# Two transformer blocks on one core: the routing query's norm factor moves from a VectorE multiply into the exponent, and the routing indices stay integers

## The chip, the cores and the metric

The kernel runs on one core of a Trainium2 chip. The metric is the device time of one execution in microseconds (us); smaller is better. Five engines run side by side, each working through its own list of instructions in a fixed order: TensorE (PE: matrix multiplies; its loads of stationary operands are counted apart, as PEld), VectorE (DVE), ScalarE (ACT), GpSimd (POOL) and SyncE (SP, which issues most transfers). An instruction that needs another engine's result waits for a semaphore, and all that stands behind it on its own engine waits with it.

## The reference

One sequence of 512 tokens, width 1024, goes through two transformer blocks in float32. The change lies in the last part of the second block, a feed-forward layer that picks 128 of 16,384 experts for each token. Cut to that part:

```python
def peer(h, w_pq, sub_keys, u_emb, v_emb):          # h: the normalised input, 512 x 1024
    q = (h @ w_pq).reshape(B, S, 8, 2, 128)         # 8 heads, two half-queries each
    sc = jnp.einsum("bshcd,hcnd->bshcn", q, sub_keys)        # 128 scores for each half
    s_top, i_top = lax.top_k(sc, 16)
    cand = s_top[..., 0, :, None] + s_top[..., 1, None, :]   # 16 x 16 sums
    cand_idx = i_top[..., 0, :, None] * 128 + i_top[..., 1, None, :]
    ...
    best, pos = lax.top_k(cand, 16)
    expert_idx = jnp.take_along_axis(cand_idx, pos, axis=-1)
    gate = jax.nn.softmax(best, axis=-1)
    ...
    a = gelu(einsum("ced,cd->ce", u_emb[idx], hx))           # per chunk of 128 tokens
    return einsum("ce,ced->cd", g * a, v_emb[idx])
```

The normalised input is h = x * r * g, where r is one factor for each token (one over the root mean square) and g a gain for each of the 1024 columns. r is positive, so scores with and without it have the same order within a token.

## The kernel before

**Weights.** Every matrix product runs over weight units w0 to w435 of 128x1024. A unit is brought from HBM by SP, two units to a transfer, and split into a high part (`w..h`, an ACT copy) and a low part (`w..l`, a subtraction); a product is then three matmuls (hi*lo, lo*hi, hi*hi). There are three buffers for split units, so a unit's copy on ACT may run only a little ahead of PE. The low part is made on DVE, or, for units 180 to 307 while the planner's flag `gates_on` is off, on POOL (`lo_eng`).

**Routing.** w164 to w179 are the 16 products `pq{h}{c}` (8 heads, two halves), 128x512 in PSUM with the queries along the partitions and the tokens along the columns. Each is carried to SBUF as `pqs` by a DVE multiply with `rr[1]`, the factors r spread over all partitions (`n4r` in the trace). For each head `head_lists` makes the 128 scores of 512 tokens on PE (`sk`), copies them to SBUF on ACT (`skc`), and finds the 16 best of each half with `top16` on DVE: for each of four token blocks two rounds of MAX8 and FIND_INDEX8, with a MATCH_REPLACE8 between them. The positions come as 32-bit integers in `iu` and are cast to bfloat16 in `itop_`. `pqs` and `skc` share a pool of seven 128x512 buffers (`t2`).

**From lists to gates.** `block_best(b)`, b = 0 to 3, takes one block of 128 tokens: it adds candidate scores, picks the best 16, takes the positions apart, looks up the list indices with a one-hot product (`eq`, 128x1024, four times a block), and makes the softmax gate (`best`, `bsum`, `IJG`). Block 0 goes by rows: for each of 128 choices a gathered row of U and of V (POOL gathers, `last`/`row<-in_un` and `in_vn`; DVE reduces, printed as ISA or CUSTOM). Blocks 1 to 3 go by dense tables: `gates()` turns IJG round on PE (`ijg`), splits it into bfloat16 parts (`ijb`, `grest`), and for every 8 tokens builds five one-hot tiles on DVE (`hot`, a set of five; a name such as `hot_3120` is block 3, token 120, and a set's buffers are two deep, one of the five only one). From each set PE makes two groups `gp` of 12 small matmuls (4 tokens each), ACT copies a group to `stage`, and every fourth group a 1 MB transfer `g_dr` writes the table out. All in all 48 sets and 96 groups. Meanwhile PE runs the products `u` over w180 to w307 (24 matmuls of 128x384 to a unit), whose results are multiplied with the tables and with w308 to w435 in the last stage (`acc`).

**What sets the order.** All engines' lists are fixed when the program is built, by a planner. `Clock` keeps a modelled time for each engine; `Merge` runs the main line (weights and products) and weaves in steps of the side lines: `ls` (head lists, block_best, gates, one after the other), `rw` (rows), `ln` (norms). A step of a side line says when it is due: `room("V", 1.5)` is the time at which modelled DVE work has shrunk to 1.5 us ahead. The modelled price of a DVE operation is

```python
two = all(x.dtype == BF16 for x in (out, *ins))
return 0.07 + n / (1920 if two else 960)
```

for n elements a partition. One place ends the weaving: before the product of w304 (`o == NOCT - 1 and j == 4` in `peer_u`) `yield ("ls",)` lets out all that is left of the lists and gates, without a product between.

Of the kernel before, what the change touches and what calls it, by code (L numbers as in the profile page):

```python
# [10 lines left out]
F32 = mybir.dt.float32  # L11
F32R = mybir.dt.float32r
BF16 = mybir.dt.bfloat16
I32 = mybir.dt.int32
U32 = mybir.dt.uint32
AF = mybir.ActivationFunctionType
ALU = mybir.AluOpType
# [4 lines left out]
P = 128  # L22
# [3 lines left out]
NB = 4  # L26
# [164 lines left out]
def body(tc, a):  # L191
# [5 lines left out]
    with ExitStack() as ctx:  # L197
# [121 lines left out]
        wk = mkpool(ph, "wk")  # L319
# [4 lines left out]
        def t2(name, dt=F32):  # L324
            return wk.tile([P, T], dt, tag="t2", name=name, bufs=NT2)
# [228 lines left out]
        rr = []  # L554
# [205 lines left out]
        for g in range(2):  # L760
            c = 64 * g
# [318 lines left out]
        def u_rows():  # L1080

            due = clk.free["PE"]
            while rows[0] < P:
# [2 lines left out]
                due = max(due + PACE, clk.free["PE"] - 2 * PACE)  # L1086
                row_step()
                yield due
        iota = wk.tile([P, P], F32, name="iota")
        G.iota(iota, pattern=[[1, P]], base=0, channel_multiplier=0, allow_small_or_imprecise_dtypes=True)  # L1090
        iota2 = wk.tile([P, P, 2], BF16, name="iota2")
        V.tensor_copy(iota2, iota[:, :, None].to_broadcast([P, P, 2]))


        stop_ = wk.tile([P, 2, NB, 8, 16], F32, name="stop_")
        itop_ = wk.tile([P, 2, NB, 8, 16], BF16, name="itop_")
        iu = wk.tile([P, NB, 16], U32, name="iu")
        IJG = wk.tile([P, NB, 3, P], F32, name="IJG")
        iota16 = wk.tile([P, 16, 16], BF16, name="iota16")
        V.tensor_copy(iota16, iota[:, 0:16, None].to_broadcast([P, 16, 16]))  # L1100

        def top16(vals, idx, x):

            V.max(vals[:, 0:8], x)
            V.max_index(idx[:, 0:8], vals[:, 0:8], x)
            V.match_replace(x, vals[:, 0:8], x, -3.0e38)
            V.max(vals[:, 8:16], x)
            V.max_index(idx[:, 8:16], vals[:, 8:16], x)
# [10 lines left out]
        def head_lists(h, qs):  # L1119
            sk = skeys.pop(0)  # L1120
            load_sk(h + 2)
            yield at(*qs)
            for c in range(2):
                s_ = psd(f"sk{h}{c}")
                for b in range(NB):
                    PE.matmul(s_[:, b * P:(b + 1) * P], qs[c][:, b * P:(b + 1) * P], sk[:, c, :],
                              start=True, stop=True)
                sc = t2(f"skc{h}{c}")
                S.activation(sc, s_, AF.Copy)
                yield room("V", 1.5, sc)  # L1130
                for b in range(NB):
                    top16(stop_[:, c, b, h], iu[:, b], sc[:, b * P:(b + 1) * P])
                    yield room("V", 1.5)
                V.tensor_copy(itop_[:, c, :, h], iu)

# [4 lines left out]
        def block_best(b):  # L1142

            s0, s1 = stop_[:, 0, b], stop_[:, 1, b]
            ca = wk.tile([P, 8, NCAND], F32, tag="ca", name=f"ca{b}", bufs=1)
            for rows, cols, part in ((slice(0, NFULL), 16, ca[:, :, :NC1]), (slice(NFULL, 16), 4, ca[:, :, NC1:])):
                n = rows.stop - rows.start
                V.tensor_tensor(part.rearrange("p h (i j) -> p h i j", j=cols),
                                s0[:, :, rows, None].to_broadcast([P, 8, n, cols]),
                                s1[:, :, None, :cols].to_broadcast([P, 8, n, cols]), ALU.add)  # L1150
            best = wk.tile([P, 2, 8, 16], F32, tag="best", name=f"best{b}", bufs=1)
            pos = wk.tile([P, 5, 8, 16], U32, tag="pos", name=f"pos{b}", bufs=1)
            for h in range(8):
                top16(best[:, 0, h], pos[:, 0, h], ca[:, h])
                yield room("V", 1.5)

            V.tensor_tensor(best[:, 1], best[:, 0], best[:, 0, :, 0:1].to_broadcast([P, 8, 16]), ALU.subtract)
            S.activation(best[:, 1], best[:, 1], AF.Exp)
            gates_on[0] = True

            for k, (n, op) in enumerate(((4, ALU.logical_shift_right), (15, ALU.bitwise_and),
                                         (2, ALU.logical_shift_right), (3, ALU.bitwise_and))):
                V.tensor_scalar(pos[:, 1 + k], pos[:, 0], n, None, op)
            far = wk.tile([P, 8, 16], F32, tag="far", name=f"far{b}", bufs=1)
            V.tensor_scalar(far, pos[:, 0], float(NC1), None, ALU.is_ge)
            d = wk.tile([P, 2, 8, 16], F32, tag="dpos", name=f"dpos{b}", bufs=1)
            V.scalar_tensor_tensor(d[:, 0], pos[:, 3], float(NFULL - NC1 // 4), pos[:, 1], ALU.add, ALU.subtract)
            V.tensor_tensor(d[:, 1], pos[:, 4], pos[:, 2], ALU.subtract)
            V.tensor_tensor(d, d, far[:, None].to_broadcast([P, 2, 8, 16]), ALU.mult)
            ab = wk.tile([P, 2, 8, 16], BF16, tag="pab", name=f"pab{b}", bufs=1)  # L1170
            V.tensor_tensor(ab, d, pos[:, 1:3], ALU.add)
            yield room("V", 1.5)
            for c in range(2):

                for h in (slice(0, 4), slice(4, 8)):
                    eq = wk.tile([P, 4, 16, 16], BF16, tag="eq", name=f"eq{b}{c}{h.start}", bufs=1)
                    V.tensor_tensor(eq, ab[:, c, h, None, :].to_broadcast([P, 4, 16, 16]),
                                    iota16[:, None].to_broadcast([P, 4, 16, 16]), ALU.is_equal)
                    V.tensor_tensor(eq, eq, itop_[:, c, b, h, :, None].to_broadcast([P, 4, 16, 16]), ALU.mult)
                    for n in (8, 4, 2):  # L1180
                        V.tensor_tensor(eq[:, :, :n], eq[:, :, :n], eq[:, :, n:2 * n], ALU.add)
                    V.tensor_tensor(IJG[:, b, c].rearrange("p (h k) -> p h k", h=8)[:, h], eq[:, :, 0], eq[:, :, 1],
                                    ALU.add)
                    yield room("V", 1.5)
            sm = wk.tile([P, 2, 8], F32, tag="bsum", name=f"bsum{b}", bufs=1)
            V.tensor_reduce(sm[:, 0], best[:, 1], axis=AX.X, op=ALU.add)
            V.reciprocal(sm[:, 1], sm[:, 0])
            V.tensor_tensor(IJG[:, b, 2].rearrange("p (h k) -> p h k", h=8), best[:, 1],
                            sm[:, 1, :, None].to_broadcast([P, 8, 16]), ALU.mult)
            gates_on[0] = False  # L1190
            if b == 0:
                V.scalar_tensor_tensor(eid, IJG[:, 0, 0], float(P), IJG[:, 0, 1], ALU.mult, ALU.add)
                V.tensor_copy(eg, IJG[:, 0, 2])
                mg.spawn("rw", u_rows())
            yield room("V", 1.5)
# [63 lines left out]
        def peer_u():  # L1259
            mg.spawn("ln", rms_steps(acc, "n4", rr))  # L1260
            for h in range(8):
                qs = []
                for c in range(2):
                    o = yield from linear(hp, f"pq{h}{c}")
                    if h + c == 0:
                        yield ("ln",)
                        mg.spawn("ln", norm2())
                    t = t2(f"pqs{h}{c}")
                    V.tensor_tensor(t, o, rr[1], ALU.mult)
                    qs.append(t)  # L1270
                mg.spawn("ls", head_lists(h, qs))
            yield ("ln",)
            hp.clear()
            cur_n.clear()

            for i in range(2):
                s_ = slot(f"last{i}").rearrange("p k t -> p (k t)")
                acts.append(s_[:, :KT * TD].rearrange("p (k t) -> p k t", k=KT))
                bufs_.append(s_[:, KT * TD:])
            bufs_.extend(rowp.tile([P, D], F32, name=f"row{i}") for i in range(NROW - 2))  # L1280
            for b in range(NB):
                mg.spawn("ls", block_best(b))
            mg.spawn("ls", gates())
            for o in range(NOCT):
                ao = acts[o % 2]
                if o >= NOCT - NRES:
                    aocts[o] = ao
                for j in range(8):
                    if o == NOCT - 1 and j == 4:
                        yield ("ls",)  # L1290
                        last_phase()
                    if o == NOCT - 1 and j == 7:
                        for i in range(WAHEAD):
                            list(weighted(i))
                    r = yield from linear(h2, f"u{o}{j}")
                    S.activation(ao[:, j], r[:, P:], AF.Gelu)
                if o < NOCT - NRES:
                    nc.scalar.dma_start(a_dr[o], ao)
# [242 lines left out]
```

## Time and profile before

| | us |
|---|---|
| median of 3 runs | 2441.09 |
| lowest, highest | 2439.46, 2441.44 |
| profiled execution, its own time | 2439.86 |
| its span in the trace | 2437.8 |
| PE busy in it | 2364.7 (97%) |
| DVE busy in it | 1759.3 (72%) |
| ACT, POOL busy in it | 1036.0 (42%), 741.0 (30%) |

The trace holds every instruction of one execution with its start, its duration and what it waited for. The views used below are sums of busy time by stretch, groups of like instructions, timelines of one engine, and the list of PE's waits. "Granted clock" (PEclk) is TensorE's clock in a stretch as a share of its full speed of 2.4 GHz; 0.50 is its lower level of 1.2 GHz.

### The profile page before, as it was taken

The numbers are of one execution on the slowest core, as the hardware profiler recorded it, in microseconds if no ns is written. First come the engines' busy times: TensorE is split into PE (matmuls) and PEld (weight loads), VectorE is DVE, ScalarE is ACT, GpSimd is POOL, SyncE is SP. The second block draws the span as 40 slices with busy tenths as digits, with TensorE's granted clock in tenths as the row PEclk, the third lists the DMA queues.
The fourth block names the chain that finished last, engine by engine and source line by source line (L and its number), as shares of the span: only waits on it lengthen the run. The fifth ranks groups of instructions, "written<-read, shape, count | busy, mean of one in ns | idle before, by whom it ended". The sixth has DMA issues, their size and how long they took to land.

```text
span 2437.8 us, 33926 instructions
## 1 busy us (share of the span) xinstructions
PE 2364.7 (97%) x13114; PEld 2111.2 (87%) x13121; DVE 1759.3 (72%) x3167; ACT 1036.0 (42%) x1558; POOL 741.0 (30%) x586
## 2 busy tenths in 40 slices
PE   9999999999999889999999999999998999999997
PEld 7777888888776667777889999999997999999997
DVE  4637644443357789755789898999996888888874
ACT  4454433232246456444324334455554333333333
POOL 2122011110126578401233455333322332323211
PEclk9999999999999999999999999999999999999998
DMA  4110222222211112222224788899998999999972
GB/s 169 57 54 35 91 97 93 104 87 104 87 67 55 52 53 87 87 87 91 93 94 173 292 316 301 313 327 347 345 323 265 360 359 364 353 362 355 372 292 85
DMA packets 141857, 466.14 MB, mean 191 GB/s; under 512 B 10624, under 2 KB 61952, under 8 KB 112000
## 3 DMA queue, kind: packets, MB, share of 16 engines
q1 hardware_dynamic: 52416, 281.04, 31.5%
q0 software_dynamic: 36864, 134.23, 15.5%
q10 hardware_dynamic: 52416, 48.70, 5.9%
q8 instruction: 103, 1.69, 0.3%
q14 instruction: 58, 0.48, 0.1%
HBM read 414.65 MB, written 49.28 MB: 190 GB/s over the span
## 4 chain that ended last, share of the span: by engine, by line
PE 66%; issue 14%; DVE 10%; POOL 4%; ACT 3%; DMA 2%; SPq 0%; POOLq 0%; DVEq 0%; ACTq 0%
PE acc L134 22%; PE u L134 9%; PE up L134 5%; PE gate L134 5%; PE pq L134 3%; PE wo L134 2%; PE qkb L134 2%; DVE hot L134 2%; PE co L134 2%; PE gc L134 2%; POOL row L1054 1%; POOL last L1054 1%; PE ga L134 1%; PE ao L134 1%; DVE cyp L134 1%
## 5 line engine op out<-in xcount | busy, mean ns | idle before, releaser
L134 POOL TENSOR_TENSOR cy<-cy,cvt 128x511 f32<-128x511 f32 (+14 forms) x120 | 173.5, 1445 | 69.7 <-ACT cvt L134 59.1
L134 ACT ACTIVATE last<-u 128x384 f32<-128x384 f32 x128 | 63.0, 492 | 226.1 <-PE u L134 225.9
L1054 POOL DMA_INDIRECT last<-in_un,eid x64 | 80.5, 1257 | 167.9 <-DVE ea L134 131.4
L1054 POOL DMA_INDIRECT last<-in_vn,eid x64 | 70.8, 1106 | 198.9 <-DVE yt L134 188.6
L1054 POOL DMA_INDIRECT row<-in_un,eid x64 | 82.3, 1285 | 136.4 <-DVE ea L134 133.5
L1054 POOL DMA_INDIRECT row<-in_vn,eid x64 | 74.1, 1158 | 153.5 <-DVE yt L134 143.6
L134 ACT ACTIVATE stage<-gp 128x512 f32<-128x512 f32 x96 | 95.9, 1110 | 8.0 <-PE gp L134 8.0
L134 DVE TENSOR_TENSOR hot<-hot,ijb 128x1024 bf16<-128x1024 bf16 x144 | 91.0, 686 | 1.5
L134 PE MATMUL gp<-hot,hot 128*128 128x128 bf16 x1152 | 76.0, 221 | 14.1 <-ACT last L134 6.7
L134 PEld LDWEIGHTS <-hot 128*128 128x128 bf16 x1152 | 67.5, 98 | 24.0 <-DVE hot L134 19.6
L134 DVE SCALAR_TENSOR_TENSOR cyp<-u,par,cyp 128x511 f32<-128x511 f32 (+28 forms) x116 | 85.3, 735 | 2.4
L134 DVE CUSTOM_DVE_ANT_0 last<-last,h2tok 128x1024 f32<-128x1024 f32 x64 | 77.2, 1212 | 10.6 <-DMA last<-in_un,eid 10.6
L134 DVE SCALAR_TENSOR_TENSOR yt<-last,ea,yt 128x1024 f32<-128x1024 f32 x63 | 80.5, 1278 | 2.1 <-DMA last<-in_vn,eid 2.1
L134 DVE SCALAR_TENSOR_TENSOR yt<-row,ea,yt 128x1024 f32<-128x1024 f32 x64 | 81.8, 1278 | 0.1
L134 DVE CUSTOM_DVE_ANT_0 row<-row,h2tok 128x1024 f32<-128x1024 f32 x64 | 77.2, 1213 | 5.7 <-DMA row<-in_un,eid 5.3
L134 ACT ACTIVATE cvt<-u,par 128x511 f32<-128x511 f32 (+14 forms) x120 | 78.9, 700 | 0.0
L134 DVE TENSOR_TENSOR wv<-last,goct 128x384 f32<-128x384 f32 x128 | 70.5, 551 | 0.0
L134 DVE TENSOR_TENSOR hot<-iota,ijb 128x1024 bf16<-128x1024 bf16 x96 | 61.7, 683 | 0.0
L134 DVE TENSOR_TENSOR su<-up,n2r 128x512 f32<-128x512 f32 x22 | 15.2, 691 | 51.8 <-PE up L134 51.8
L134 PEld LDWEIGHTS o<-v,pT 128*128 128x128 f32 x224 | 29.6, 199 | 18.4 <-DVE pT L134 10.9
L134 PE MATMUL o<-v,pT 128*128 128x64 f32 x224 | 31.8, 284 | 10.7 <-DVE pT L134 7.6
L134 DVE MAX8 stop__8676<-skc 128x8 f32<-128x128 f32 x128 | 36.8, 287 | 5.5 <-ACT skc L134 3.2
(6459 smaller groups left out, 8465.9 us busy)
## 6 DMA issues: line engine op xcount, KB each, us to landing
raw<-in_w SPq DMA_DIRECT2D x89, 1024.0 KB, 4.8
raw<-in_u SPq DMA_DIRECT2D x64, 1024.0 KB, 7.4
raw<-in_v SPq DMA_DIRECT2D x64, 1024.0 KB, 7.2
g_dr<-stage ACTq DMA_DIRECT2D x24, 1024.0 KB, 8.4
goct<-g_dr SPq DMA_DIRECT2D x64, 384.0 KB, 8.8
a_dr<-last ACTq DMA_DIRECT2D x14, 1536.0 KB, 9.9
last<-a_dr SPq DMA_DIRECT2D x56, 384.0 KB, 10.3
xT<-in_x_t SPq DMA_DIRECT2D x1, 1024.0 KB, 9.5
```

The source lines that it names most:

```text
L134: return f(*args, **kw)
L1054: nc.gpsimd.indirect_dma_start(row_buf(n), None, t, bass.IndirectOffsetOnAxis(ap=eid[:, n % P:n % P + 1], axis=0))
```

## The change

The queries are carried to SBUF by a plain ACT copy, without r. The lists are then made on scores without r, and r comes in where `best` goes through the exponential on ACT, as its scale, one value for each token (a token is a partition there). FIND_INDEX8 writes into `itop_`, now of 32-bit integers, and the 16 casts and `iu` are gone, so the `eq` product has one bfloat16 and one 32-bit operand. The mask `far` and one 128x256 product become two operations of 128x128 that compare and multiply. `iota` borrows a `t2` buffer until it has been read.

```diff
--- before.py
+++ after.py
@@ -1086,18 +1086,18 @@
                 due = max(due + PACE, clk.free["PE"] - 2 * PACE)
                 row_step()
                 yield due
-        iota = wk.tile([P, P], F32, name="iota")
+        iota = t2("iota")[:, :P]
         G.iota(iota, pattern=[[1, P]], base=0, channel_multiplier=0, allow_small_or_imprecise_dtypes=True)
         iota2 = wk.tile([P, P, 2], BF16, name="iota2")
         V.tensor_copy(iota2, iota[:, :, None].to_broadcast([P, P, 2]))
 
 
         stop_ = wk.tile([P, 2, NB, 8, 16], F32, name="stop_")
-        itop_ = wk.tile([P, 2, NB, 8, 16], BF16, name="itop_")
-        iu = wk.tile([P, NB, 16], U32, name="iu")
+        itop_ = wk.tile([P, 2, NB, 8, 16], U32, name="itop_")
         IJG = wk.tile([P, NB, 3, P], F32, name="IJG")
         iota16 = wk.tile([P, 16, 16], BF16, name="iota16")
         V.tensor_copy(iota16, iota[:, 0:16, None].to_broadcast([P, 16, 16]))
+        iota = None
 
         def top16(vals, idx, x):
 
@@ -1129,9 +1129,8 @@
                 S.activation(sc, s_, AF.Copy)
                 yield room("V", 1.5, sc)
                 for b in range(NB):
-                    top16(stop_[:, c, b, h], iu[:, b], sc[:, b * P:(b + 1) * P])
+                    top16(stop_[:, c, b, h], itop_[:, c, b, h], sc[:, b * P:(b + 1) * P])
                     yield room("V", 1.5)
-                V.tensor_copy(itop_[:, c, :, h], iu)
 
 
 
@@ -1155,18 +1154,17 @@
                 yield room("V", 1.5)
 
             V.tensor_tensor(best[:, 1], best[:, 0], best[:, 0, :, 0:1].to_broadcast([P, 8, 16]), ALU.subtract)
-            S.activation(best[:, 1], best[:, 1], AF.Exp)
+            S.activation(best[:, 1], best[:, 1], AF.Exp, scale=rr[0][:, b:b + 1])
             gates_on[0] = True
 
             for k, (n, op) in enumerate(((4, ALU.logical_shift_right), (15, ALU.bitwise_and),
                                          (2, ALU.logical_shift_right), (3, ALU.bitwise_and))):
                 V.tensor_scalar(pos[:, 1 + k], pos[:, 0], n, None, op)
-            far = wk.tile([P, 8, 16], F32, tag="far", name=f"far{b}", bufs=1)
-            V.tensor_scalar(far, pos[:, 0], float(NC1), None, ALU.is_ge)
             d = wk.tile([P, 2, 8, 16], F32, tag="dpos", name=f"dpos{b}", bufs=1)
             V.scalar_tensor_tensor(d[:, 0], pos[:, 3], float(NFULL - NC1 // 4), pos[:, 1], ALU.add, ALU.subtract)
             V.tensor_tensor(d[:, 1], pos[:, 4], pos[:, 2], ALU.subtract)
-            V.tensor_tensor(d, d, far[:, None].to_broadcast([P, 2, 8, 16]), ALU.mult)
+            for c in range(2):
+                V.scalar_tensor_tensor(d[:, c], pos[:, 0], float(NC1), d[:, c], ALU.is_ge, ALU.mult)
             ab = wk.tile([P, 2, 8, 16], BF16, tag="pab", name=f"pab{b}", bufs=1)
             V.tensor_tensor(ab, d, pos[:, 1:3], ALU.add)
             yield room("V", 1.5)
@@ -1265,8 +1263,9 @@
                     if h + c == 0:
                         yield ("ln",)
                         mg.spawn("ln", norm2())
+
                     t = t2(f"pqs{h}{c}")
-                    V.tensor_tensor(t, o, rr[1], ALU.mult)
+                    S.activation(t, o, AF.Copy)
                     qs.append(t)
                 mg.spawn("ls", head_lists(h, qs))
             yield ("ln",)
```

PE's list has the same 13,330 entries before and after. The places at which side work stands change on all engines. The planner's price of an `eq` product goes from 0.07 + 1024/1920 = 0.60 to 0.07 + 1024/960 = 1.14 us, since its operands are no longer all BF16. With that one price left at 0.60 the changed code is built with its `bsum` and `gp` at the old places.

**ACT at the end of the routing products.** Names: `w179h` to `w183h` are high parts of weights, `skc` copies of scores, `last<-u` results of the first products behind the routing. Before:

```order
L134 ACTIVATE w179h<-raw_9212 128x1024
L134 ACTIVATE skc_9387<-sk_9382 128x512
L134 ACTIVATE w180h<-raw_9304 128x1024
L134 ACTIVATE w181h<-raw_9304 128x1024
L134 ACTIVATE skc_9467<-sk_9462 128x512
L134 ACTIVATE w182h<-raw_9398 128x1024
L134 ACTIVATE skc_9546<-sk_9541 128x512
L134 ACT_TABLE_LOAD
L134 ACTIVATE last_9504<-u_9508 128x384
L134 ACTIVATE w183h<-raw_9398 128x1024
```

After:

```order
L134 ACTIVATE pqs_9338<-pq_9290 128x512
L134 ACTIVATE w179h<-raw_9198 128x1024
L134 ACTIVATE pqs_9379<-pq_9340 128x512
L134 ACTIVATE w180h<-raw_9291 128x1024
L134 ACTIVATE skc_9395<-sk_9390 128x512
L134 ACTIVATE pqs_9436<-pq_9381 128x512
L134 ACTIVATE w181h<-raw_9291 128x1024
L134 ACTIVATE skc_9462<-sk_9457 128x512
L134 ACTIVATE pqs_9489<-pq_9438 128x512
L134 ACTIVATE w182h<-raw_9382 128x1024
L134 ACTIVATE skc_9537<-sk_9532 128x512
L134 ACT_TABLE_LOAD
```

The last four query copies now stand among the high parts of w179 to w182. `pqs_9338` waits for head 3's first scores on PE, which stand behind the product of w177; the other three wait for a `t2` buffer until DVE has finished a list: `pqs_9379` that of head 2's second half, `pqs_9436` that of head 3's first, `pqs_9489` that of head 3's second half. On DVE w179's low part stands in the middle of the list of head 2's second half, with two of its four blocks behind it. On PE the scores of head 3's second half stand within the product of w179 and those of head 4's first half within that of w180, before and after.

**DVE where block 3's routing ends**, before (the gate is finished behind the low part of w252) and after (behind that of w268). `ISA` with `ea` is a row reduce:

```order
L134 TENSOR_TENSOR w252l<-raw_12317,w252h 128x1024
L134 ISA last_9504,ea<-last_9504,h2tok 128x1024
L134 ISA ea 128x1
L134 TENSOR_REDUCE bsum_12416<-best_11847 128x8
L134 RECIPROCAL bsum_12416<-bsum_12416 128x8
L134 TENSOR_TENSOR IJG<-best_11847,bsum_12416 128x128
```

```order
L134 TENSOR_TENSOR w268l<-raw_12832,w268h 128x1024
L134 TENSOR_REDUCE bsum_12920<-best_12158 128x8
L134 RECIPROCAL bsum_12920<-bsum_12920 128x8
L134 TENSOR_TENSOR IJG<-best_12158,bsum_12920 128x128
L134 ISA last_9492,ea<-last_9492,h2tok 128x1024
```

The four places of `bsum` are behind w204l, w221l, w237l and w252l before, and behind w205l, w226l, w247l and w268l after. On POOL the low part of w205 stood behind the first four row gathers; it is now on DVE, and w206l stands there. The turning of block 1, 2 and 3 on PE (`ijg`) was behind the products of w251, w268 and w286 and is behind those of w266, w284 and w302.

**DVE at the end of the gates**, from the low part of w305 on. Before:

```order
L134 TENSOR_TENSOR w305l<-raw_15780,w305h 128x1024
L134 TENSOR_TENSOR hot_3120_16033<-iota_8674,ijb_14930 128x1024
L134 TENSOR_TENSOR hot_3120_16034<-iota_8674,ijb_14930 128x1024
L134 TENSOR_TENSOR hot_3120_16035<-hot_3120_16034,ijb_14930 128x1024
L134 TENSOR_TENSOR hot_3120_16036<-hot_3120_16034,ijb_14930 128x1024
L134 TENSOR_TENSOR hot_3120_16037<-hot_3120_16034,ijb_14930 128x1024
L134 ISA row_9507,ea<-row_9507,h2tok 128x1024
L134 ISA ea 128x1
L134 TENSOR_TENSOR ea<-ea,eg 128x128
L134 TENSOR_TENSOR w306l<-raw_15926,w306h 128x1024
```

After:

```order
L134 TENSOR_TENSOR w305l<-raw_15189,w305h 128x1024
L134 TENSOR_TENSOR grest_15439<-ijg_15434,ijb_15438 128x128
L134 TENSOR_TENSOR ijb_15438<-grest_15439,ijb_15438 128x128
L134 ISA last_9492,ea<-last_9492,h2tok 128x1024
L134 ISA ea 128x1
L134 ISA row_9493,ea<-row_9493,h2tok 128x1024
L134 ISA ea 128x1
L134 TENSOR_TENSOR hot_30_15463<-iota_8674,ijb_15438 128x1024
L134 TENSOR_TENSOR hot_30_15464<-iota_8674,ijb_15438 128x1024
L134 TENSOR_TENSOR hot_30_15465<-hot_30_15464,ijb_15438 128x1024
L134 TENSOR_TENSOR hot_30_15466<-hot_30_15464,ijb_15438 128x1024
L134 TENSOR_TENSOR hot_30_15467<-hot_30_15464,ijb_15438 128x1024
```

Before, one set of one-hots (the last, of token 120) and one row are left when w305l has been made, and then the low part of w306. Now all 16 sets of block 3 stand behind w305l, from `grest`, the splitting of block 3's gates, on, with seven rows among them, and w306l behind the 16th. On PE the 96 groups were spread from behind w254 to behind w303, four of them behind w303. Now 64 groups stand from behind w270 to behind w302, and 32 behind w303, ahead of the product of w304, with no product between them.

## Rows read from the trace of the kernel before

**Rows 1.** The page: the span, and each engine's busy time, share and instructions.

```profile
span 2437.8 us, 33926 instructions
...
PE 2364.7 (97%) x13114; PEld 2111.2 (87%) x13121; DVE 1759.3 (72%) x3167; ACT 1036.0 (42%) x1558; POOL 741.0 (30%) x586
```

**Rows 2.** Busy us by stretch: PE, PEld, DVE, ACT, POOL, then PEclk, DMA share, GB/s.

```profile
1550.00:1870.00 320.00, 304.72 (x2480) 293.99 (x2478) 298.22 (x455) 173.98 (x212) 103.83 (x78) 0.99 0.95 323
...
1870.00:1884.00 14.00, 9.13 (x50) 8.29 (x48) 5.91 (x8) 5.99 (x11) 0.00 (x0) 0.99 0.73 285
1884.00:2420.00 536.00, 535.78 (x3086) 535.30 (x3087) 430.09 (x514) 203.56 (x260) 144.88 (x128) 1.00 0.88 328
```

**Rows 3.** DVE groups, 1137 to 1560 us: count, busy us, mean ns, idle before.

```profile
L134 DVE TENSOR_TENSOR eq<-eq,itop__8677 128x1024 bf16<-128x1024 bf16 x16 | 19.6, 1225 | 0.6
...
L134 DVE TENSOR_TENSOR pqs<-pq,n4r 128x512 f32<-128x512 f32 x16 | 10.9, 682 | 13.2 <-PE sk L134 6.1 <-PE pq L134 4.0 <-ACT n4r L134 3.1
L134 DVE CAST itop__8677<-iu 128x64 bf16<-128x64 uint32 x16 | 8.3, 519 | 0.5
...
L134 DVE TENSOR_TENSOR w167l<-raw,w167h 128x1024 fp32r<-128x1024 f32 x1 | 1.2, 1226 | 0.3 <-ACT w167h L134 0.3
```

**Rows 4.** DVE's timeline, two blocks of a half-list: start us, us, engine, operation.

```profile
1219.97 0.28 DVE L134 MAX8 stop__8676<-skc 128x8 f32<-128x128 f32 x1
...
1221.68 0.28 DVE L134 MAX8 stop__8676<-skc 128x8 f32<-128x128 f32 x1
```

**Rows 5.** ACT's timeline at the routing's end; in brackets the idle time before.

```profile
1227.02 0.60 ACT L134 ACTIVATE skc<-sk 128x512 f32<-128x512 f32 x1 [8.63 <-DVE iu L134]
...
1249.81 0.60 ACT L134 ACTIVATE skc<-sk 128x512 f32<-128x512 f32 x1 [8.62 <-DVE iu L134]
...
1252.11 1.05 ACT L134 ACTIVATE w183h<-raw 128x1024 fp32r<-128x1024 f32 x1
```

**Rows 6.** PE's timeline to its two stops, same columns.

```profile
1223.53 0.39 PE L134 MATMUL pq<-norm2l,w178h 128*128 128x512 f32 x1
...
1240.50 0.33 PE L134 MATMUL u<-h2l,w181h 128*128 128x384 f32 x1
...
1253.21 0.69 PE L134 MATMUL u<-h2l,w183h 128*128 128x384 f32 x1 [3.32 <-ACT w183h L134]
1255.64 0.69 PE L134 MATMUL u<-h2h,w183l 128*128 128x384 f32 x1 [1.74 <-POOL w183l L134]
...
1356.62 0.45 PE L134 MATMUL u<-h2h,w205l 128*128 128x384 f32 x1 [2.21 <-POOL w205l L134]
```

**Rows 7.** Stretches behind both stops, columns of rows 2 (PEclk third from the end).

```profile
1252.00:1260.00 8.00, 5.05 (x17) 4.65 (x18) 7.27 (x35) 4.41 (x7) 5.19 (x3) 0.57 0.35 133
1358.00:1361.00 3.00, 3.00 (x11) 3.00 (x10) 1.28 (x3) 0.00 (x0) 3.00 (x2) 0.50 1.03 423
```

**Rows 8.** PE's waits, 1550 to 1884 us: total, times, longest us.

```profile
PE gp L134 <- ACT last L134: 6.7, 12, 0.6
PE gp L134 <- DVE hot L134: 5.9, 3, 4.8
```

**Rows 9.** DVE's timeline over the last one-hot sets.

```profile
1842.67 1.29 DVE L134 TENSOR_TENSOR hot<-iota,ijb 128x1024 bf16<-128x1024 bf16 x2
...
1845.80 1.21 DVE L134 CUSTOM_DVE_ANT_0 last<-last,h2tok 128x1024 f32<-128x1024 f32 x1
...
1855.95 1.89 DVE L134 TENSOR_TENSOR hot<-hot,ijb 128x1024 bf16<-128x1024 bf16 x3
```

**Rows 10.** PE's timeline there: the last six groups.

```profile
1845.94 1.55 PE L134 MATMUL gp<-hot,hot 128*128 128x128 bf16 x24 [0.56 <-ACT last L134]
1847.30 0.42 PE L134 MATMUL u<-h2l,w303h 128*128 128x384 f32 x1
...
1851.55 1.56 PE L134 MATMUL gp<-hot,hot 128*128 128x128 bf16 x24
1857.90 2.74 PE L134 MATMUL gp<-hot,hot 128*128 128x128 bf16 x24 [4.79 <-DVE hot L134]
```

## The prediction

> **What bounds the kernel now.** I read the page first: PE is busy 97% of the span [rows 1], so a change can pay only where PE stands still, and it can cost wherever it makes PE wait. Then busy time by stretch. In the last stage PE works 535.78 of 536 us [rows 2]: nothing done earlier can shorten that, it can only start sooner or later. From 1550 to 1870 us, where tables and products run together, PE works 304.72 of 320 us with DVE at 298.22 [rows 2]: PE leads, with DVE close behind. The list of PE's waits there gives 6.7 us in twelve short waits for ACT and 5.9 us for one-hot tiles, 4.8 of these in a single wait [rows 8], the last pair of groups of all [rows 10]. Ahead of that the timeline has two stops: 3.32 + 1.74 us for w183's parts and 2.21 us for w205's low part [rows 6], each with a piece at the lower clock behind it: 0.57 granted over 8 us, 0.50 over 3 [rows 7]. So all that DVE's lighter work could give back lies in some 13 us of waits and 3 us of slow clock.
>
> **The change, part by part.** *What leaves DVE.* The query multiplies are 16 x 682 ns = 10.9 us, the casts 16 x 519 ns = 8.3 us [rows 3], together 19 us. None of it lies on PE's path as such: PE's two stops in that stretch are for ACT and POOL [rows 6]. It counts only through what DVE's lists let go.
>
> *The `eq` product with a 32-bit operand.* No row shows this form. With two bfloat16 operands it takes 1225 ns, and a float32 subtraction of the same 1024 elements takes 1226 [rows 3]: there is no fast rate to lose, so I take 1225, from 1225 to twice that for the range (0 to +19.6 us on DVE, in blocks that DVE makes while PE has products). The Trainium skill, "VectorE: DVE Perf Modes", section "Mode 2×_1P — pack two bf16 into one 32-bit read", gives two results a cycle only where every operand has 16 bits and step one; read for the operand's width alone, it speaks against this change, as an estimate 16 x 0.6 = 10 us of DVE. The row at the float32 rate says that the product had not been in that mode (its index operand is repeated along the innermost axis), so the sum holds nothing for it. The two small operations for `far` cost as much as those they replace, within a microsecond; the scale of the exponential is free.
>
> *Term A, the end of the routing.* The query copies now stand in ACT's list among the weight copies. ACT takes its list in order: at 1249.81 a score copy waited 8.62 us for DVE, and w183h ran only behind it [rows 5]. The Trainium skill, "Perfetto Trace Analysis", section "Tensor Engine Instruction (MATMUL, LD_WEIGHTS)", calls the queues of ACT, DVE and GpSimd strictly first in, first out; by that rule a weight copy can't pass a waiting query copy, without it this term would be 0, and the trace agrees with the rule.
> The walk, with a copy at 0.60, a weight copy at 1.05 [rows 5], a block of a list at 1.71 [rows 4], a DVE low part at 1.22 [rows 3] and a POOL one at 2.4 (1253.21 to 1255.64 [rows 6]): the scores ahead of w178 end at 1223.5 [rows 6]; the first of the four copies ends at 1224.1, w179h at 1225.1, its low part on DVE at 1226.3, the two blocks behind it at 1229.7, the second copy at 1230.3, w180h at 1231.4, the scores at 1232.0, four blocks at 1238.8, the third copy at 1239.4, w181h at 1240.5 and its low part at 1242.8. PE comes to w181 at 1240.50 [rows 6]: 2.2 us of waiting. The same once more: scores 1241.0, blocks 1247.9, fourth copy 1248.5, w182h 1249.5, low part 1251.9; PE is through with w181 at 1246.8 and waits 2.7 + 2.2 us. w183 is then ready at 1255.4, ahead of PE at 1256.7. So two stops of 7.1 us in all come in place of one of 5.1, and a slow piece behind each in place of one: 0.43 x 8 us less what was idle in it, about 1.6 us [rows 6, 7]. Sum +3.5. The bounds: 0, if lists without queries and casts among them end sooner than walked, to +8, if w183 is late as well.
>
> *Term B, w205.* Its low part was made on POOL behind four row gathers and PE waited 2.21 us, with 1.7 us behind it at half clock [rows 6, 7]. It is now on DVE, ahead of `bsum`; what POOL makes behind the gathers is w206's, a product of 4.2 us later. -3.9; bounds -3.9 and 0 (w206 takes its place).
>
> *Term C, the order of the tables.* This is the large one, and it comes from a price, not from work: the planner counts an `eq` product at 1.14 in place of 0.60 us, so each block's gate is finished later, block 3's behind w268 in place of w252. The tables then run out of products to hide under: 32 groups stand behind w303, where four did.
> Where block 3's sets can begin: the last group of block 2, and the turning of block 3, stand behind w302. In the trace the last group of all ends at 1857.90 + 2.74 = 1860.6 [rows 10]. The products and groups ahead of that point are the same; 4.25 us for w303 (1847.30 to 1851.55) and 16 pairs of groups at 1.36 (1845.94 to 1847.30) [rows 10], 26.0 us together, now come behind block 2's last group. Idle time up to there was 15.3 us [rows 2]; without the last wait, and for 64 groups in place of 92, 10.5 x 64/92 = 7.3, which is 8.0 less. The slow clock of the last pair takes off 1.4 more. Block 2 is done at 1860.6 - 26.0 - 8.0 - 1.4 = 1825.
> Behind it DVE must get the turned gates (three copies at 0.60, w305l 1.22, two rows of 1.21 and two small operations, with hand-overs some 7 us [rows 3, 5, 9]): the first set begins near 1832. A set takes 3.13 us (1842.67 to 1845.80 [rows 9]); 16 of them and the five rows between them are 50.1 + 6.0 us. The last set ends near 1888, in place of 1855.95 + 1.89 = 1857.8 [rows 9]. PE has those 26 us of work for the 63 us from 1825 on and stands still for the rest. What follows the last set (groups, ACT, the table's transfer, the start of the last stage) is the same chain, so **C = +30.5**. The bounds: +21, with no idle time at all among the 64 groups (-7.3) and the first set 2 us sooner; +38.5, with the whole 15.3 us there. The chain behind could give back up to the 4.9 us that PE idles from 1870 to 1884 [rows 2], where weights come earlier.
> What hides nothing here: two sets at most can be built ahead, since the one-hot buffers are two deep, and the first needs the turning of block 3 anyway. The 19 us that DVE saved lie 550 us back in fixed lists; the list says which instruction follows which, so a DVE that is early there waits at the next weight.
>
> **Sum.** The profiled execution took 2439.86 us, 1.2 under the median. 2439.86 + 3.5 - 3.9 + 30.5 = 2470.0; from the median, 2471.
>
> **The rivals.** *Relief wins (faster).* DVE is the neighbour that PE waits for, and 19 us go from it. If the tables' order cost nothing, the two stops with their slow clock (5.1 + 1.6 + 3.9) and the one-hot waits (5.9) could go: 2441 - 16.5 = 2424.5. It decides at term C: block 3's first set would have to begin by 1802, some 30 us ahead of my walk. For it: DVE's 298 us of 320. Against it: the turning of block 3 is behind w302 on PE, whatever DVE does.
> *The tail is hidden after all (same).* The 30 us would have to be paid back by idle time elsewhere: all of the 15.3 us, term B and the 4.9 us, which is 24: 2447. For it: each of these is in the rows. Against it: the 15.3 us are mostly short waits of groups for ACT [rows 8], and the groups don't go away.
> *The table's transfers end last (worse).* Eight 1 MB writes now fall into 56 us, and two `stage` buffers let one write overlap one filling. DMA is at a share of 0.95 from 1550 to 1870 [rows 2], though no more weights but two pairs are wanted in the tail. If each pair of sets had to wait a microsecond for a buffer, that is +8: 2479; with w183 late too, 2484.
> *The change doesn't reach the order.* If the price mattered nowhere, A and B alone would be left: 2441. The listing of the built program excludes it.
>
> **How the numbers follow.** Forecast 0.78, the transfers 0.10, the hidden tail 0.05, relief 0.07. The forecast's own range goes from 2441 + 0 - 3.9 + 21 - 4.9 = 2453 to 2441 + 8 + 0 + 38.5 = 2487; with both corners trimmed a little, 2455 to 2485, which takes in the worse rival and leaves out relief, the hidden tail and some of the corners. A measurement of this kernel can tell 0.2%, 4.9 us, from no change. Faster: relief, 0.07. Same: half of the hidden tail, 0.03. Slower: the rest, 0.90.
>
> **What would show it.** A: PE waits for ACT at w181h and w182h instead of w183h. B: no wait at w205l. C: 16 sets in a row on DVE at 3.1 us each, with PE under half busy beside them and waiting for `hot` some 16 times, the last stage starting near 1914 in place of 1884 and taking its 536 us as before. It is wrong if the sets are ahead of the products, if the last stage starts within 10 us of before, or if a set takes clearly less than 3.1 us when PE isn't busy.

## The result, and the profile after

The changed kernel takes 2466.29 us (median of 4 runs, 2464.13 to 2469.82) against 2440.4 us for the kernel before on the same chip: ratio 1.0111, 95% interval 1.0098 to 1.0123, so 26 us or 1.1% slower. The forecast was 2471, with a range of 2455 to 2485.

The page of the changed kernel, span and busy time of each engine, answers to [rows 1]:

```profile
span 2463.8 us, 33933 instructions
...
PE 2366.5 (96%) x13121; PEld 2114.2 (86%) x13121; DVE 1746.1 (71%) x3137; ACT 1044.5 (42%) x1574; POOL 723.2 (29%) x584
```

DVE is busy 13 us less and PE 2 us more, and the span is 26 us longer. Where the time went is shown by busy time by stretch (columns as in [rows 2]: PE, PEld, DVE, ACT, POOL, PEclk, DMA share, GB/s):

```profile
1320.00:1550.00 230.00, 230.00 (x1329) 230.00 (x1328) 195.08 (x482) 90.26 (x120) 99.21 (x72) 1.00 0.81 297
1550.00:1870.00 320.00, 290.71 (x2293) 282.02 (x2292) 299.49 (x475) 162.15 (x200) 100.08 (x80) 0.96 0.91 311
...
1910.00:2446.00 536.00, 535.63 (x3076) 535.05 (x3077) 429.78 (x512) 203.66 (x259) 143.65 (x127) 0.99 0.87 328
```

From 1320 to 1550 us PE has no idle time left at all: the stop at w205 is gone. From 1550 to 1870 it idles 29.3 us where it idled 15.3, and the last stage, still 536 us and full, starts 26 us later. PE's waits say which end costs what (total, times, longest), first from 1137 to 1560 us, then from 1550 to 1920:

```profile
PE u L134 <- POOL w183l L134: 2.0, 1, 2.0
PE u L134 <- POOL w181l L134: 2.0, 1, 2.0
PE u L134 <- POOL w182l L134: 2.0, 1, 2.0
PE u L134 <- ACT w182h L134: 0.9, 1, 0.9
...
PE u L134 <- ACT w181h L134: 0.8, 1, 0.8
PE u L134 <- ACT w183h L134: 0.3, 1, 0.3
...
PE gp L134 <- DVE hot L134: 32.6, 15, 9.2
...
PE gp L134 <- ACT last L134: 3.4, 6, 0.6
PE gp L134 <- ACT stage L134: 1.6, 1, 1.6
```

Three stops in place of one at the end of the routing, 8.0 us in all; and 32.6 us of waiting for one-hot tiles where [rows 8] had 5.9.

The tail in two timelines of the changed kernel (start us, us, engine, operation; in brackets the idle time before), DVE first:

```profile
1829.21 1.22 DVE L134 CUSTOM_DVE_ANT_0 row<-row,h2tok 128x1024 f32<-128x1024 f32 x1 [2.12 <-DMA row<-in_un,eid]
1830.36 1.29 DVE L134 TENSOR_TENSOR hot<-iota,ijb 128x1024 bf16<-128x1024 bf16 x2
...
1833.49 1.29 DVE L134 TENSOR_TENSOR hot<-iota,ijb 128x1024 bf16<-128x1024 bf16 x2
...
1885.05 1.90 DVE L134 TENSOR_TENSOR hot<-hot,ijb 128x1024 bf16<-128x1024 bf16 x3
```

```profile
1818.31 1.55 PE L134 MATMUL gp<-hot,hot 128*128 128x128 bf16 x24 [0.56 <-ACT last L134]
...
1833.63 2.74 PE L134 MATMUL gp<-hot,hot 128*128 128x128 bf16 x24 [9.25 <-DVE hot L134]
...
1844.46 2.74 PE L134 MATMUL gp<-hot,hot 128*128 128x128 bf16 x24 [5.76 <-DVE hot L134]
...
1852.54 2.74 PE L134 MATMUL gp<-hot,hot 128*128 128x128 bf16 x24 [3.29 <-DVE hot L134]
...
1858.80 1.55 PE L134 MATMUL gp<-hot,hot 128*128 128x128 bf16 x24 [0.47 <-DVE hot L134]
...
1887.01 1.55 PE L134 MATMUL gp<-hot,hot 128*128 128x128 bf16 x24 [1.58 <-DVE hot L134]
...
1910.37 0.80 PE L134 MATMUL acc<-wv0l,w308h 128*128 128x512 f32 x1 [3.61 <-ACT last L134]
```

Block 2's last pair of groups starts at 1818.31. The first set of block 3 begins at 1830.36, the next 3.13 us later, the sixteenth ends at 1886.95; from 1865 us on a pair of groups takes PE 1.55 us and then it waits 1.58 for the next set. The kernel before had its last set done at 1857.8 [rows 9].

**The difference, stretch by stretch.** In the table below each time runs between the first matmuls of two weights in the profiled execution, so it holds busy time and stops alike. It is used for every experiment too. What lies ahead of w164 isn't touched by any of these kernels; w164 begins at 1133.9 to 1140.0 us in their profiles. Single executions differ by that much ahead of it, so the stretches are compared and not the spans; each stretch is of one execution.

| | w164 to w184 (routing and its end) | w184 to w254 (lists, gates) | w254 to w308 (tables) | w308 to the end |
|---|---|---|---|---|
| before | 124.6 | 300.2 | 321.9 | 553.6 |
| changed | 129.7 | 295.8 | 347.4 | 553.4 |
| difference | +5.1 | -4.4 | +25.5 | -0.2 |

The first three differences are terms A, B and C in turn. With the last, they make up +26.0, the whole difference of the two spans.

### The profile page after: what moved, and what is told of

It is laid out like the page before. It is cut to its first block, busy times and chain, and to the rows that moved or that the text cites. A ratio compares the mean times of both kernels' runs of the same rounds, so it can differ in the third digit from the quotient of the medians.

```text
span 2463.8 us, 33933 instructions
## 1 busy us (share of the span) xinstructions
PE 2366.5 (96%) x13121; PEld 2114.2 (86%) x13121; DVE 1746.1 (71%) x3137; ACT 1044.5 (42%) x1574; POOL 723.2 (29%) x584
## 4 chain that ended last, share of the span: by engine, by line
PE 70%; issue 14%; DVE 7%; POOL 4%; ACT 3%; DMA 1%; SPq 0%; POOLq 0%; DVEq 0%; ACTq 0%
PE acc L134 22%; PE u L134 14%; PE up L134 5%; PE gate L134 5%; PE pq L134 3%; DVE hot L134 2%; PE wo L134 2%; PE qkb L134 2%; PE co L134 2%; PE gc L134 2%; POOL row L1054 1%; POOL last L1054 1%; PE ga L134 1%; PE ao L134 1%; DVE cyp L134 1%
## 5 line engine op out<-in xcount | busy, mean ns | idle before, releaser
L1054 POOL DMA_INDIRECT last<-in_un,eid x64 | 75.4, 1178 | 155.9 <-DVE ea L134 128.7
L1054 POOL DMA_INDIRECT row<-in_un,eid x64 | 74.8, 1169 | 150.1 <-DVE ea L134 146.5
L134 PE MATMUL gp<-hot,hot 128*128 128x128 bf16 x1152 | 79.9, 227 | 37.6 <-DVE hot L134 32.6
L134 DVE MAX8 stop__8676<-skc 128x8 f32<-128x128 f32 x128 | 36.8, 288 | 26.1 <-ACT skc L134 23.9
```

The lines of the kernel that those rows point to most:

```text
L134: return f(*args, **kw)
L1054: nc.gpsimd.indirect_dma_start(row_buf(n), None, t, bass.IndirectOffsetOnAxis(ap=eid[:, n % P:n % P + 1], axis=0))
```

## The experiments

Two theories stood against each other. *Order*: the work on the chip hardly matters; the new price of the `eq` product moves the tables (B and C), and the query copies in ACT's list hold up weights (A). *Work*: the new forms themselves cost the time, or DVE's relief pays once something else is taken away. Each kernel ran beside the kernel before. Their stretches, in the columns of the table above:

| | w164 to w184 | w184 to w254 | w254 to w308 | w308 to end | median us | ratio, 95% interval |
|---|---|---|---|---|---|---|
| old price | 129.7 | 300.8 | 324.4 | 553.6 | 2445.87 | 1.0024 (1.0015 to 1.0034) |
| price only | 125.7 | 295.8 | 347.7 | 553.5 | 2460.42 | 1.0080 (1.0067 to 1.0093) |
| queries only | 131.6 | 300.4 | 321.3 | 553.4 | 2445.38 | 1.0030 (1.0019 to 1.0042) |
| queries on DVE | 125.3 | 295.8 | 347.7 | 553.7 | 2460.52 | 1.0089 (1.0076 to 1.0102) |
| price 0.90 | 129.5 | 295.8 | 332.4 | 553.0 | 2448.39 | 1.0039 (1.0026 to 1.0052) |
| indices only | 125.0 | 299.5 | 321.2 | 552.5 | 2438.57 | 1.0003 (0.9994 to 1.0011) |
| last four on DVE | 124.9 | 300.5 | 321.1 | 552.9 | 2438.36 | 1.0001 (0.9993 to 1.0010) |
| w205 on DVE | 125.3 | 304.0 | 319.7 | 553.4 | 2440.46 | 1.0001 (0.9992 to 1.0010) |
| hot at 0.57 | 125.4 | 296.1 | 324.9 | 553.5 | 2438.16 | 0.9998 (0.9989 to 1.0007) |
| hot at 0.53 | 124.7 | 296.2 | 332.3 | 550.8 | 2443.48 | 1.0014 (1.0005 to 1.0023) |

The kernel before had medians of 2440.56 us beside the first four, 2438.76 beside the next group (price 0.90, indices only, last four, w205) and 2439.48 beside the last two.

**1. The whole change at the old price.** To the changed kernel's planner:

```diff
-            two = all(x.dtype == BF16 for x in (out, *ins))
+            two = all(x.dtype == BF16 or (x.dtype == U32 and out.dtype == BF16) for x in (out, *ins))
```

> The whole change, with one line of the planner more: an eq product with a 32-bit index operand is priced at 0.60 us as before. The work on the chip is that of the changed kernel; the places of bsum and of the 96 groups are those of before (4 behind w303). Order theory: term C goes (-25 us), w205's low part is on POOL again behind the gathers (its stop of 2.2 us and the slow piece come back, +4), the stops at w181 to w183 stay: 2440.4 + 5.1 = about 2445.5 us. Work theory (the 32-bit operand, the lists without casts or the queries cost the time themselves): 2460 to 2466 us.

2445.87 us, as the order theory has it: 20 of the 26 us are gone with one number that no engine executes. The tail is back to one wait of before's size (PE's waits of this kernel, 1840 to 1910 us):

```profile
PE gp L134 <- DVE hot L134: 4.8, 1, 4.8
```

The gain of term B is gone too (300.8 us, where the kernel before has 300.2), but not by the one stop of 2.2 us at w205 that was expected. This kernel's waits from 1137 to 1560 us have two:

```profile
PE u L134 <- DVE w215l L134: 2.2, 1, 2.2
...
PE u L134 <- POOL w205l L134: 1.1, 1, 1.1
```

**2. The price alone, in the kernel before.**

```diff
-            two = all(x.dtype == BF16 for x in (out, *ins))
+            two = all(x.dtype == BF16 for x in (out, *ins)) and not any(x.tensor.name.startswith("itop") for x in ins)
```

> The kernel before, with the planner's price of the eq product alone raised from 0.60 to 1.14 us; no instruction is changed, only places. 32 groups then stand behind w303. Order theory: no stop at w205 (-4.1), the 16 sets of block 3 laid bare (+25.1): 2440.4 + 21 = about 2461 us, with the stop at w183 as before (5 us). Work theory: 2440 us.

2460.42 us. The kernel before, with the same work on the same data, loses 20 us to the order alone (one low part goes from POOL to DVE with it). Its waits, from 1137 to 1560 us and then from 1560 to 1920, show the stop at w183 of before, none at w205, and the tail of the changed kernel:

```profile
PE u L134 <- ACT w183h L134: 3.3, 1, 3.3
PE u L134 <- POOL w183l L134: 2.0, 1, 2.0
...
PE gp L134 <- DVE hot L134: 34.4, 16, 9.4
```

Runs 1 and 2 undo and do the same thing, and both give the stretches B and C of the other kernel to within 2.5 us.

**3. The queries alone, in the kernel before.**

```diff
-            S.activation(best[:, 1], best[:, 1], AF.Exp)
+            S.activation(best[:, 1], best[:, 1], AF.Exp, scale=rr[0][:, b:b + 1])
-                    V.tensor_tensor(t, o, rr[1], ALU.mult)
+                    S.activation(t, o, AF.Copy)
```

> The kernel before with one part of the change: queries carried by an ACT copy without the factor, which goes into the exponent's scale. Casts, far and iota stay as before; bsum and the groups stand where they stood. Theory of ACT's queue: weight copies of w181 and w182 wait behind query copies that wait for lists, +5 us: 2445.5 us, PE stopped at w181, w182 and w183 instead of w183 alone. Relief theory (DVE without the 10.9 us of query multiplies lets lists end sooner): 2434 to 2440 us, with one stop or none.

2445.38 us, +4.8: the 10.9 us of query multiplies are gone from DVE and the kernel is slower, with the stops where ACT's queue puts them (PE's waits, 1137 to 1560 us):

```profile
PE u L134 <- ACT w182h L134: 2.4, 1, 2.4
PE u L134 <- POOL w205l L134: 2.3, 1, 2.3
PE u L134 <- POOL w181l L134: 2.0, 1, 2.0
PE u L134 <- POOL w183l L134: 2.0, 1, 2.0
PE u L134 <- POOL w182l L134: 2.0, 1, 2.0
```

The first stretch is 1.9 us longer than in run 1, where the casts are gone as well (131.6 and 129.7); the medians of the two kernels don't show that difference.

**4. The changed kernel with the query copies on DVE.**

```diff
-                    S.activation(t, o, AF.Copy)
+                    V.tensor_copy(t, o)
```

> The changed kernel with the query copies, still without the factor, on DVE in place of ACT; the tables' order is that of the changed kernel (32 groups behind w303). Theory of ACT's queue: the stops at w181 and w182 go and one at w183, as before or shorter, is left: 2466.3 - 5 = 2461 us, the same as raising the price alone. If the lists rather than ACT's queue cause these stops: 2466 us.

2460.52 us, the time of run 2. The stops at w181 and w182 are gone, that at w183 is left as it was before:

```profile
PE u L134 <- ACT w183h L134: 3.3, 1, 3.3
PE u L134 <- POOL w183l L134: 2.0, 1, 2.0
```

So term A is ACT's queue and not the lists. It also shows that the stop at w183 doesn't come from the casts or from r: both are gone here and it is the same.

**5. A price between.** 0.90 us for the `eq` product leaves 14 groups behind w303.

> The changed kernel with the eq product priced at 0.90 us, between the old 0.60 and the new 1.14: 14 groups (7 sets) stand behind w303, in place of 4 or 32; w205's low part is on DVE as in the changed kernel, the queries on ACT. Order theory: the stop ahead of w304 grows with the sets left: 8.9 us for 2 sets before, 5 sets of 3.13 more less their groups that no longer stand elsewhere (5 x 1.36) and some idle time among those: C about +8. 2440.5 + 5.1 - 4.2 + 8 = 2449 us. If C comes from elsewhere than the tail's length, 2441 or 2466 us.

2448.39 us, 9.6 over the kernel before, where 8.5 was expected. The tables' stretch grows with the sets that stand behind w303: 321.9 us with 2 sets, 332.4 with 7, 347.4 with 16: 2.1 us a set, then 1.7. The waits of this kernel for hot tiles, 1840 to 1910 us, lie between too:

```profile
PE gp L136 <- DVE hot L136: 14.4, 6, 3.9
```

**6. What is left of the change without its two costs.** Old price and queries on DVE:

> The changed kernel with the old price (0.60) and with the query copies on DVE, without the factor: so the integer indices without casts, the shorter far, and the factor in the exponent are left, in the order of before. Theory that DVE's relief lies under PE's work: 2440.5 us, with the stops at w183 (5.3 us) and w205 (2.2 us) as before. Relief theory (8.3 us of casts less, lists end sooner): 2432 to 2436 us.

2438.57 against 2438.76 us: no difference. 16 casts fewer, 8.3 us of DVE [rows 3], bring nothing that can be measured.

**7. Only the last four query copies on DVE**, old price:

```diff
-                    S.activation(t, o, AF.Copy)
+                    if h < 6:
+                        S.activation(t, o, AF.Copy)
+                    else:
+                        V.tensor_copy(t, o)
```

> The changed kernel with the old price and only the last four query copies (heads 6 and 7) on DVE, the first twelve on ACT. Theory that only those copies hurt which wait for lists among the last weight copies of the routing: no stop at w181 and w182, 2440.5 us. If any query copy on ACT costs: 2443 to 2446 us.

2438.36 us, no difference from before, where the same kernel with all 16 on ACT (run 1) takes 5 us more. Twelve copies on ACT are free, though one of them waits 4.80 us for a list too; the price is for the last four, which stand among the last weight copies. Twelve multiplies and 16 casts, 16.5 us by [rows 3], are gone from DVE here, and the time is the same.

**8. w205 on DVE**, queries on DVE, `eq` at 0.30 us so that the groups keep their places (only the line for w205 is shown):

```diff
-            return G if NU_BASE <= i < NU_BASE + 128 and not gates_on[0] else V
+            return G if NU_BASE <= i < NU_BASE + 128 and i != 205 and not gates_on[0] else V
```

> The same with w205's low part on DVE in place of POOL behind the gathers, and the eq product priced at 0.30 us so that the groups keep their old places (4 behind w303). If the stop at w205 is POOL's queue and nothing else: 4.2 us less than the version with the indices only: 2436 us, with one stop (w183) left before the tables.

2440.46 us: the expectation was wrong. The stop moved to w207. Here POOL's timeline of this kernel, and behind it PE's:

```profile
1356.88 2.42 POOL L136 TENSOR_TENSOR w206l<-raw,w206h 128x1024 fp32r<-128x1024 f32 x1
1359.46 0.96 POOL L1056 DMA_INDIRECT last<-in_un,eid  x1 [0.16 <-issue]
1366.21 0.94 POOL L1056 DMA_INDIRECT last<-in_un,eid  x1 [5.79 <-DVE ea L136]
1367.17 2.37 POOL L136 TENSOR_TENSOR w207l<-raw,w207h 128x1024 fp32r<-128x1024 f32 x1
```

```profile
1369.60 0.69 PE L136 MATMUL u<-h2h,w207l 128*128 128x384 f32 x1 [3.67 <-POOL w207l L136]
```

A gather that waits 5.79 us for DVE to free its row stands ahead of w207l. In the changed kernel only one gather stands between w206 and w208 on POOL, behind w207l. So w205 on DVE is not enough for term B: it also matters where the gathers fall among POOL's weights, and the changed kernel has that by its order. The traces show the place of the gathers; no run moved a gather alone.

**9 and 10. Both ends at once.** Block 0's `eq` at 1.14 us (the changed kernel's places at w205), blocks 1 to 3 at 0.30, queries on DVE, and a one-hot tile at 0.57 or 0.53 in place of 0.60 (the prices are shown, at 0.57):

```diff
+            if out.tensor.name.startswith("hot"):
+                return 0.57
+            if any(x.tensor.name.startswith("itop") for x in ins) and out.dtype == BF16:
+                return 1.14 if out.tensor.name.startswith("eq0") else 0.3
```

> The changed kernel with the query copies on DVE and three prices of the planner set apart: an eq product of block 0 at 1.14 us (its gate is finished behind w205l, so POOL isn't asked for w205), those of blocks 1 to 3 at 0.30, a one-hot tile at 0.57 in place of 0.60. 2 groups stand behind w303. Order theory: the gain at w205 is kept (-4.2) and the tail is a set shorter than before (about -2): 2438.8 - 6 = 2433 us. If the stop at w205 only moves to another weight on POOL, as with w205 alone on DVE: 2437 to 2440 us.

> The same with a one-hot tile at 0.53 us: the last group stands behind w298, none behind w303. If the tail's stop is only the order, it goes whole (8.9 us ahead of w304 before): 2438.8 - 4.2 - 7 = 2428 us. If DVE is the limit of that stretch (298 us busy of 320), PE waits among the groups instead for hot tiles and low parts: 2433 to 2440 us.

At 0.57: 2438.16 us, no difference, where 2433 was expected. It lies in the range named for a stop that only moves, but no such stop is there: the gain at w205 is kept (296.1), and the tables' stretch grows by 3.0 (324.9). At 0.53: 2443.48 us, 4.0 slower and above both expectations; the tables' stretch is 332.3 although no group is left behind w303. PE's waits for hot tiles, 1560 to 1920 us, at 0.57 and then at 0.53:

```profile
PE gp L138 <- DVE hot L138: 14.9, 22, 1.1
...
PE gp L138 <- DVE hot L138: 24.9, 29, 1.4
```

Many short waits in place of one long one. Groups that the plan puts closer together than DVE makes sets wait one by one. No version that was run is faster than the kernel before beyond its interval.

## Why the prediction was right, step by step

**What bounds it.** Right: the last stage was 536 us of PE before and after, and the loss lies ahead of it.

**What leaves DVE.** Right: the multiplies and casts, 19 us by [rows 3], went, and nothing came of them (runs 4, 6 and 7). DVE's busy time fell by 13 us and not by 19; two low parts more, 2.4 us, are among what came to it. The scale of the exponential, taken as free, is small: those four operations on ACT took 402 ns each in place of 311, 0.4 us together. In the trace the saving turned into waiting. The groups of DVE operations, 1137 to 1560 us, answer to [rows 3]; the first line is of the kernel before, the others of the changed one:

```profile
L134 DVE MAX8 stop__8676<-skc 128x8 f32<-128x128 f32 x128 | 36.8, 287 | 5.5 <-ACT skc L134 3.2
...
L134 DVE MAX8 stop__8676<-skc 128x8 f32<-128x128 f32 x128 | 36.8, 288 | 26.1 <-ACT skc L134 23.9
...
L134 DVE TENSOR_TENSOR eq<-eq,itop__8677 128x1024 bf16<-128x1024 bf16 x12 | 14.7, 1225 | 0.4
```

23.9 us of idle time ahead of MAX8, until ACT had copied the scores, where it was 3.2 (and 13.2 ahead of the query multiplies [rows 3]): ACT waits for the lists, and the lists for ACT. The last row settles the price of the new form: 1225 ns with a 32-bit operand, the same as with two bfloat16 ones. The value taken was right, and nothing of the range above it was needed. The Trainium skill, "VectorE: DVE Perf Modes", section "Mode 2×_1P — pack two bf16 into one 32-bit read", asks for 16-bit operands of step one; the trace agrees, 1225 ns where the index operand is repeated along the innermost axis, whatever its type, beside 686 ns for the comparison that fills `eq` (`eq<-pab,iota`), of the same size with 16-bit operands of step one.

**Term A**, +3.5 forecast, +5.1 measured, inside its bounds of 0 to 8. The walk held to within 0.8 us (ACT's timeline of the changed kernel):

```profile
1239.58 0.60 ACT L134 ACTIVATE pqs<-pq 128x512 f32<-128x512 f32 x1 [7.13 <-DVE itop__8677 L134]
1240.07 1.05 ACT L134 ACTIVATE w181h<-raw 128x1024 fp32r<-128x1024 f32 x1
...
1248.73 0.60 ACT L134 ACTIVATE pqs<-pq 128x512 f32<-128x512 f32 x1 [7.12 <-DVE itop__8677 L134]
1249.22 1.05 ACT L134 ACTIVATE w182h<-raw 128x1024 fp32r<-128x1024 f32 x1
1256.43 0.60 ACT L134 ACTIVATE skc<-sk 128x512 f32<-128x512 f32 x1 [6.16 <-PE sk L134]
...
1258.73 1.05 ACT L134 ACTIVATE w183h<-raw 128x1024 fp32r<-128x1024 f32 x1
```

Both query copies waited 7.1 us for a list, and the weight copies ran right behind them. The third query copy ended at 1240.2 (walked: 1239.4), w181h at 1241.1 (1240.5), w182h at 1250.3 (1249.5). What was missed is the third stop: w183 was to be ready ahead of PE, and PE waited 0.3 + 2.0 us for it. The walk put the score copy ahead of w183h right behind w182h; it waited 6.16 us for scores that PE makes within the product of w182, which was late itself, and w183h ran behind it.

**Term B**, -3.9 forecast, -4.4 measured: right in size. Its reason was only half of it. The prediction had w205 on DVE as the cure; in run 8, with that and a lower price of `eq`, the stop is two weights on.

**Term C**, +30.5 forecast, +25.5 measured, with its mechanism as described (runs 1, 2 and 5). What was mis-sized in it is the point where block 2 is done and what surrounds it. Busy time from 1550 us to the product of w303 in the kernel before, and to the end of block 2's last pair in the changed one:

```profile
1550.00:1847.30 297.30, 286.80 (x2360) 276.46 (x2359) 286.32 (x437) 166.60 (x203) 98.69 (x75) 1.00 0.97 331
...
1550.00:1819.70 269.70, 265.36 (x2026) 259.00 (x2026) 252.44 (x397) 140.53 (x175) 87.81 (x70) 1.00 0.94 326
```

- Block 2's last pair was to end at 1825; it ended at 1819.7 (1818.31 and 1.36 for a pair). The idle time among the 64 groups was put at 7.3 us by scaling 10.5; it was 4.3, as the waits of groups for ACT had halved (six in place of twelve). And the 14 pairs that no longer stand ahead of w303 were put at 1.36 us each, 19.0 together; PE's busy time is 21.4 less.
- The first set was to begin 7 us behind that; it took 10.7. DVE was busy to 1825.0 with w304l, three rows and w305l, and 2.12 us are a row's transfer that it waited for (timeline above).
- 16 sets and five rows: 56.1 us forecast, 56.6 measured (1830.36 to 1886.95). Last set done at 1887.0, where 1888 was forecast.
- The chain behind was taken as the same; it was 3.0 us shorter (1886.95 to 1910.37 is 23.4 us, from 1857.84 to 1884.21 it was 26.4), which the prediction had allowed for only in its range. The last pair of groups ran at the full clock, 1.55 us, where it took 2.74 [rows 10], and so did the product behind it: 2.4 of the 3.0 us.

That the sum came within 5 us is luck in part: A was 1.6 too small and C 5.0 too large, and within C the early end of block 2 and the late first set pull against each other.

**The rivals.** Relief is excluded by runs 6 and 7, which keep the order of before; run 3 can't tell, since ACT's queue costs there. The transfers of the tables did not set the pace: ACT waited twice for a `stage` buffer to be written out, 2.2 us in all, and PE had one wait for the `stage` copies, of 1.6 us. The tail was not hidden.

## What to carry to other kernels

Where a planner fixes the order, a change's price in the planner is part of the change: here a type moved a price by 0.54 us, and the order that followed cost 21 us while the operation itself cost the same 1225 ns. Read the order for what ends up behind the last work that could cover it, and price that by the row of the engine that must then work alone. Before work is moved to an engine with room, look at what its queue holds behind the place: a copy that waits for a buffer stops the weight copies behind it. Four of sixteen cost 5 us so; the other twelve, whose waits were 4.8 us at most, were free.

## What the runs showed that was not expected

In the tail the granted clock fell and came back while PE was busy about half of the time (busy time by stretch of the changed kernel, PEclk third from the end):

```profile
1826.00:1860.00 34.00, 15.67 (x165) 14.36 (x166) 31.23 (x53) 12.25 (x15) 7.28 (x7) 0.65 0.70 232
1860.00:1888.00 28.00, 13.75 (x217) 12.20 (x215) 26.67 (x43) 17.48 (x19) 0.00 (x0) 1.00 0.67 186
```

PE works 46% of the first stretch and 49% of the second. In the first its long gaps are 9.25, 5.76 and 3.29 us (PE's timeline above) and the clock is 0.65 on the mean; in the second it works 1.55 us and rests 1.58, and the clock is at its full level. Also worth a note: the kernel's price for `eq`, 0.60 us, was further from the measured 1225 ns than the new 1.14, and the truer price gave the worse order.
